# Linear attention's weights by pairs of heads, and sample attention's steps by twos, in a hybrid decoder layer on one core

## The chip, the core and the metric

One NeuronCore of a Trainium2 chip runs the whole layer as one program. Its engines run side by side: TensorE (PE; PEld is its weight load), VectorE (DVE), ScalarE (ACT), GpSimd (POOL) and SyncE (SP), which here issues most DMAs. The metric is the device time of one execution in microseconds (us), lower is better.

## What is computed

One layer serves 1024 prompt tokens and 8 sequences of 8 sample tokens (64 sample tokens, 1088 in all), model width 1024:

```python
h = macaron_half(x, ...)                 # SwiGLU feed-forward 1, half weight
fq, fk, fv, logf, gq, gk, gv, gg, log_a = project(rmsnorm(h), w_in, ...)
fo = fox_prompt(fq, fk, fv, logf)        # 8 heads x 64, softmax with forget bias
     # the sample tokens instead attend to 16 cached pages of 128 keys and values each
go = gla_prompt(gq, gk, gv, log_a)       # 4 heads, key 64, value 128, linear attention
h = h + rmsnorm(merge(fo, go, gg, ...))  # go is normed, times silu(gg); then w_out
y = macaron_half(h, ...)                 # feed-forward 2
```

In the linear attention the weight of key position s for query position t is the sum over the 64 key channels of `q[t] * k[s] * exp(b[t] - b[s])` for s <= t, with `b` the running sum of the log decay.

## The kernel before

**Projections by three products.** Activations and weights are split in a high and a low part (type fp32r), and every product is three matmuls a 128-row block of the inner dimension: `gemm` (line 210) for w_in, w_out and the gate and up halves of the feed-forwards, `down` (line 440) for the down half. One `gemm` over 512 tokens is 8 inner blocks of 3 matmuls. Weights come as blocks of 512 KB through `Feed`: two raw tiles, then three split ones (`wh`, `wl`), in the order of use.

**Background work in pieces.** Attention is a Python generator that the projections advance while they are written out. After each inner block, `tick` adds a planned time, 0.42e-3 us per matmul column, and for `rate` times that time it calls `piece`, which advances the generator to its next `yield`. A block over 512 tokens counts 3 x 512 x 0.42e-3 = 0.645 planned us. A planner then fixes each engine's order by priority (order of writing) and by when it believes operands to be there. What of the generator is left at a fixed place is written out at once by `finish_bg`.

**Stages.** (1) feed-forward 1; (2) w_in for the first 512 tokens; (3) `start3`: the rest of w_in, with prompt attention for tokens 0 to 511 beside it (`fox` over 16 pairs of a 256-query chunk and a head; `gla` over four tiles of 128 tokens, held back until `hook3`), rate RATE0 = 1.1, finished at `mid3`; (4) w_out for those tokens; (5) `start4`: feed-forward 2 for the first 512 tokens. Its groups G0 (two blocks of 128 hidden columns) and G1 to G4 (four blocks each) take gate and up first, then down. Beside them runs `second`: first `sample` at rate RATES = 1.1, then at RATE1 = 2.6 `fox` and `gla` for tokens 512 to 1023 and the sample tokens (`gla` tiles 4, 5, 8, 6, 7; 8 is the sample tile), taking turns by `together`, which yields after every step of either. At its end `second` loads the mixed heads back from DRAM (`mixd` to `p4.y`, line 1388) and splits them into `ub` in eight pieces. `mid4` calls `finish_bg` after G4's down, and (6) w_out for the last 576 columns starts there, which reads `ub`; (7) feed-forward 2 ends.

**Linear attention of one tile.** `gla_prep` makes for each of seven levels (64, 32, ... 1; three for the sample tile) the decays E, their exponential on ACT, and multiplies k into one half of each level's columns and q into the other (line 1166). `gla_mid` has for two levels at a time, and for each half e of the 128 partitions (two heads stand in a tile's two halves), the matmuls `pa` (line 1209) of 64 rows: stationary E's 128 columns, moving its 64 query columns. A masked copy puts them into `at` (line 1212). Then it yields. The operands are plain fp32, and the trace has two passes of each such matmul. `gla_post` multiplies with the values and the state, norms, and multiplies with `gg` (line 1280), which it loads at its start.

**Sample attention.** `sample` handles four pairs of sequences. `LEAD` pieces pass first; then come the steps, one to a piece: 16 key steps (K) and 16 value steps (V) a pair, each on 512 KB of cached pages (lines 837 and 875: four matmuls with 32 stationary columns, two passes each), five `turn` steps of transposes, and `scored`, `out`. K steps of the next pair alternate with V steps. Pages are fetched six steps ahead.

Of the kernel before, what the change touches and what calls it, by code (L numbers as in the profile page):

```python
# [8 lines left out]
F32 = mybir.dt.float32  # L9
# [4 lines left out]
ALU = mybir.AluOpType  # L14
# [4 lines left out]
P = 128  # L19
# [527 lines left out]
LEAD = 10  # L547
# [6 lines left out]
class StepA(Step):  # L554
    def setup_a(self):
        cp, nc = self.const, self.nc
        dr = self.dram
        self.qs = dr.tile([2, 4, P, T], F32, name="qs")
        self.ks = dr.tile([2, 4, P, T], F32, name="ks")
        self.vs = dr.tile([4, P, 2, KB, P], F32, name="vs")  # L560
        self.vss = dr.tile([4, 2, TS, P], F32, name="vss")
        self.augs = dr.tile([8, 2, TP], F32, name="augs")
        self.cns = dr.tile([2, 8, TS], F32, name="cns")
        self.afs = dr.tile([NB, 2, 8, NPG, P], F32, name="afs")
        self.gqs = dr.tile([2, P, T], F32, name="gqs")
# [6 lines left out]
        self.mixs = cp.tile([P, 4, TS], F32, name="mixs")  # L572
        self.gS = cp.tile([P, 2, P], F32, name="gS")
        self.cend = cp.tile([8, 4], F32, name="cend")

    def load_a(self):
        cp, nc, A = self.const, self.nc, self.A
        for nm, shape in (("wa2", [16, 256]), ("ba", [P, 2]), ("rst", [P, HALF + TS]), ("later", [P, P])):
            t = cp.tile(shape, F32, name=nm)
            nc.sync.dma_start(t, A[nm])  # L580
            setattr(self, nm, t)
        self.bf = cp.tile([40, 1], F32, name="bf")
        nc.sync.dma_start(self.bf[32:40, :], A["bf"])
# [67 lines left out]
    def gates(self, c0, n, pt):  # L651
# [5 lines left out]
        rs = self.rst[:, HALF:]  # L657
# [7 lines left out]
        for i in range(2):  # L665
            if i:
                yield 6.0
            z = aux("z2")
            nc.tensor.matmul(z[:, :n], self.wa2[:, i * P:(i + 1) * P], gz[:16, :n], start=True, stop=True)
            e, m = st(), st()  # L670
            nc.scalar.activation(out=e[:, :n], in_=z[:, :n], func=AF.Abs, bias=self.ba[:, i:i + 1])
            nc.scalar.activation(out=e[:, :n], in_=e[:, :n], func=AF.Exp, scale=-1.0)
            nc.scalar.activation(out=e[:, :n], in_=e[:, :n], func=AF.Ln, bias=1.0)
            nc.vector.tensor_scalar(m[:, :n], z[:, :n], self.ba[:, i:i + 1], 0.0, op0=ALU.add, op1=ALU.min)
            nc.vector.tensor_tensor(out=m[:, :n], in0=m[:, :n], in1=e[:, :n], op=ALU.subtract)
            b = e
            nc.vector.tensor_tensor_scan(out=b[:, :npr], data0=self.rst[:, :npr], data1=m[:, :npr], initial=0.0, op0=ALU.mult, op1=ALU.add)
            if npr < n:
                nc.vector.tensor_tensor_scan(out=b[:, npr:n], data0=rs, data1=m[:, npr:n], initial=0.0, op0=ALU.mult, op1=ALU.add)
            nc.sync.dma_start(self.gbs[i][:, c0:c0 + n], b[:, :n])  # L680
# [43 lines left out]
    def past_bias(self, pool):  # L724
# [4 lines left out]
        nc.sync.dma_start(idx, A["pt_col"])  # L729
        lg, inc = [big(pool.tile([P, T], F32, name=self.uid("pb"), tag="sg", bufs=2)) for _ in range(2)]  # L730
# [9 lines left out]
        nc.tensor.matmul(of[:, :8], self.later, tot, start=True, stop=True)  # L740
# [17 lines left out]
    def sample(self, X, ps):  # L758
# [5 lines left out]
        tmp = lambda nm, shape, dt: X.tile(shape, dt, name=nm, tag="ob", bufs=2)  # L764
        self.pgt = cst("pgt", [1, P], I32)
# [131 lines left out]
        def paged(kind, p, t):  # L897
            n = len(pages)
            pages.append((kind, p, t))
            steps.append(lambda: (key_step if kind == "K" else value_step)(n, p, t))  # L900

        def scored(p):
            steps.append(lambda: new_keys(p))
            steps.append(lambda: (soft(p), queries(p + 1) if p + 1 < NP else None))

        for t in range(16):
            paged("K", 0, t)
        scored(0)
        for p in range(NP):
            ks = list(range(16)) if p + 1 < NP else []  # L910
            if p == 0:
                for t in ks[:2]:
                    paged("K", 1, t)
                ks = ks[2:]
            for j in range(5):
                steps.append(lambda p=p, j=j: turn(p, j))
# [49 lines left out]
RATES = 1.1  # L966
# [18 lines left out]
class StepB(StepA):  # L985
    def setup_b(self, B):
# [18 lines left out]
        nc.gpsimd.memset(self.qe, 0.0)  # L1005
        self.qb = []
# [117 lines left out]
    def gla_prep(self, ti, B):  # L1124
# [46 lines left out]
    def gla_mid(self, ti, B):  # L1171
# [29 lines left out]
        for l0 in range(0, L, 2):  # L1201
            ls = list(range(l0, min(l0 + 2, L)))
            for e in range(2):
                pa = self.aux("pa", P, 2, 2, 64)
                vw = lambda x, l: x.rearrange("p a (k m) -> p a k m", m=2 * lev[l])[:, :, :, lev[l]:]
                for l in ls:
                    x = E[64 * e:64 * e + 64, l, :, :n]
                    for a in range(2):
                        nc.tensor.matmul(pa[:n, l - l0, a, :n // 2], x[:, a], vw(x, l)[:, a], start=True, stop=True)  # L1209
                for l in ls:  # L1210
                    mk = vw(self.lmask[:n, l + 7 - L:l + 8 - L, :n], l)[:, 0].unsqueeze(1).to_broadcast([n, 2, n // (2 * lev[l]), lev[l]])
                    nc.vector.copy_predicated(vw(at_[:, 2 * e:2 * e + 2, :], l), mk, pa[:n, l - l0, :, :n // 2].rearrange("p a (k m) -> p a k m", m=lev[l]))
                yield
        self.tile_in[ti] = (v, at, kn, el)

    def gla_post(self, ti, put, B):
# [8 lines left out]
        gg = self._gl(B, "gg", self.ggs, 4, ti * P, n)  # L1225
# [53 lines left out]
        nc.vector.scalar_tensor_tensor(out=o[:, :, :n], in0=o[:, :, :n], scalar=self.gnorm[:, :1], in1=rb[:, :, :n], op0=ALU.mult, op1=ALU.mult)  # L1279
        nc.gpsimd.tensor_tensor(out=o[:, :, :n], in0=o[:, :, :n], in1=gg, op=ALU.mult)  # L1280
# [116 lines left out]
    def whole(self):  # L1397
# [10 lines left out]
        UB, close_ub = self.pool("UB", side="right")  # L1408
        self.ub = [UB.tile([P, KB, H1N], F32R, name=f"ub{i}") for i in range(2)]
# [165 lines left out]
def consts():  # L1575
# [5 lines left out]
    r=np.ones((128,512+64),np.float32); r[:,0:512:128]=0; r[:,512::8]=0; c['rst']=r  # L1581
# [62 lines left out]
```

## Time and profile before

| | before |
|---|---|
| median of 3 runs | 2444.93 us (2437.53 to 2446.8) |
| profiled execution, its own time | 2454.03 us |
| its span, first to last instruction | 2452.3 us |
| mean granted TensorE clock | 0.983 |
| busy, share of the span | PE 98%, PEld 86%, DVE 48%, ACT 35%, POOL 15% |

Busy time is the time in which at least one instruction of an engine is open; matmuls overlap one another, so what a matmul costs is read from the distance of two starts and not from its own duration.

### The profile page before, as it was taken

The page shows a single profiled execution, that of the slowest core. Times are in us where ns is not written, and L with a number is a line of the kernel's source. Part 1 is how long each engine was busy: PE and PEld are TensorE (multiplying, and loading weights), DVE is VectorE, ACT ScalarE, POOL GpSimd, SP SyncE. Part 2 cuts the span into 40 slices and gives each one's busy share as a digit, 9 for nine tenths or more (in the row PEclk, how much of TensorE's full clock was granted, in tenths as well). Part 3 has the DMA queues.
Part 4 walks back from the last instruction along what each step waited for, and adds up shares of the span by engine and source line. Part 5 has one row for each costly group of instructions (what it writes and reads, how often), then busy time and mean ns, then how long its engine had stood idle before and what let it go on. Part 6 is the DMA issues. An engine that isn't in the chain of part 4 may idle for free.

```text
span 2452.3 us, 39759 instructions
## 1 busy us (share of the span) xinstructions
PE 2392.2 (98%) x15688; PEld 2105.6 (86%) x15688; DVE 1170.8 (48%) x2300; ACT 863.0 (35%) x1582; POOL 359.2 (15%) x418
## 2 busy tenths in 40 slices
PE   7999999999999999999999999999999999999997
PEld 7799999999999879899997555578888999999997
DVE  7223232232347765555565232357776674333345
ACT  5311211111134545555354222245454543222222
POOL 3000000000003220000124354710000321000001
PEclk9999999999999999799999999999999999999999
DMA  3111111111134576464256899856544534222222
GB/s 123 65 48 44 44 43 44 47 49 44 50 97 147 178 239 204 139 187 146 80 177 217 305 334 324 276 164 173 169 126 161 178 115 159 87 83 82 87 71 89
DMA packets 177083, 330.71 MB, mean 135 GB/s; under 512 B 25153, under 2 KB 100610, under 8 KB 176898
## 3 DMA queue, kind: packets, MB, share of 16 engines
q1 hardware_dynamic: 165234, 289.90, 36.9%
q0 software_dynamic: 11664, 38.28, 4.5%
q8 instruction: 124, 2.03, 0.3%
q14 instruction: 61, 0.50, 0.1%
HBM read 284.42 MB, written 43.69 MB: 134 GB/s over the span
## 4 chain that ended last, share of the span: by engine, by line
PE 38%; issue 4%; DVE 3%; DMA 2%; POOL 2%; ACT 1%; SPq 0%; POOLq 0%; ACTq 0%; DVEq 0%
PE mm L210 20%; PE mm L440 10%; PE sp L837 1%; PE po L875 1%; DMA wr<-in_wout 1%; PE pa L1209 1%; PE tp L1065 1%; PE po L1080 1%; DVE wl L146 1%; POOL pr L798 1%; ACT wh L145 1%; POOL y L328 0%; PE s L1047 0%; DMA pr<-in_cv,rows 0%; PE s L1048 0%
## 5 line engine op out<-in xcount | busy, mean ns | idle before, releaser
L210 PE MATMUL mm<-ub,wh 128*128 128x320 f32 (+2 forms) x3776 | 774.6, 300 | 0.1
L210 PE MATMUL mm<-ua,wh 128*128 128x512 f32 (+2 forms) x2288 | 641.8, 366 | 5.4 <-ACT wh L145 2.7
L210 PEld LDWEIGHTS mm<-ub,wh 128*128 128x128 f32 (+1 forms) x3776 | 610.5, 190 | 10.7 <-issue 3.7
L146 DVE TENSOR_TENSOR wl<-wr,wh 128x1024 fp32r<-128x1024 f32 (+1 forms) x294 | 357.8, 1217 | 449.0 <-ACT wh L145 442.2
L145 ACT CAST wh<-wr 128x1024 fp32r<-128x1024 f32 (+1 forms) x294 | 301.2, 1025 | 723.6 <-PE mm L210 309.3
L210 PE MATMUL mm<-ub,wl 128*128 128x320 f32 (+1 forms) x1872 | 554.8, 297 | 0.5 <-DVE wl L146 0.5
L210 PEld LDWEIGHTS mm<-ua,wh 128*128 128x128 f32 (+1 forms) x2288 | 400.4, 192 | 82.7 <-issue 23.3
L210 PE MATMUL mm<-ua,wl 128*128 128x512 f32 (+1 forms) x1136 | 408.8, 361 | 1.2 <-DVE wl L146 1.2
L210 PEld LDWEIGHTS mm<-ub,wl 128*128 128x128 f32 x1872 | 356.0, 190 | 0.7 <-DVE wl L146 0.7
L440 PE MATMUL mm<-hl,wh 128*128 128x256 f32 (+4 forms) x1088 | 354.3, 326 | 0.0
L440 PE MATMUL mm<-hh,wh 128*128 128x256 f32 (+2 forms) x1040 | 340.0, 328 | 1.0 <-DVE y L450 1.0
L440 PE MATMUL mm<-hh,wl 128*128 128x256 f32 (+2 forms) x1040 | 332.8, 321 | 0.0
L210 PEld LDWEIGHTS mm<-ua,wl 128*128 128x128 f32 x1136 | 217.4, 192 | 35.5 <-issue 2.7
L450 DVE TENSOR_TENSOR y<-y,mm 128x256 f32<-128x256 f32 (+2 forms) x272 | 130.0, 503 | 215.5 <-PE mm L440 215.0
L440 PEld LDWEIGHTS mm<-hl,wh 128*128 128x128 f32 (+1 forms) x1088 | 206.0, 189 | 22.1 <-issue 11.4
L440 PEld LDWEIGHTS mm<-hh,wh 128*128 128x128 f32 x1040 | 196.5, 189 | 23.2 <-issue 11.1
L224 POOL TENSOR_TENSOR ss<-ss,sq 128x256 f32<-128x256 f32 (+1 forms) x46 | 44.0, 959 | 1149.8 <-ACT sq L220 1149.2
L440 PEld LDWEIGHTS mm<-hh,wl 128*128 128x128 f32 x1040 | 196.6, 189 | 14.8 <-issue 3.7
L379 DVE TENSOR_TENSOR sg<-mm,sg 128x256 f32<-128x256 f32 (+4 forms) x112 | 55.7, 498 | 185.8 <-PE mm L210 184.3
L798 POOL DMA_INDIRECT pr<-in_cv,rows x128 | 128.3, 1003 | 98.1 <-PE po L875 41.2
L145 ACT CAST hh<-sg 128x320 fp32r<-128x320 f32 (+2 forms) x128 | 62.6, 489 | 213.1 <-DVE sg L379 170.0
L373 ACT ACTIVATE sg<-mm 128x256 f32<-128x256 f32 (+4 forms) x112 | 49.1, 439 | 143.8 <-PE mm L210 143.6
(243 smaller groups left out, 2309.5 us busy)
## 6 DMA issues: line engine op xcount, KB each, us to landing
wr<-in_wgu SPq DMA_DIRECT2D x137, 512.0 KB
wr<-in_wd SPq DMA_DIRECT2D x60, 512.0 KB
pr<-in_ck SPq DMA_DIRECT2D x112, 256.0 KB
wr<-in_win SPq DMA_DIRECT2D x50, 512.0 KB
wr<-in_wout SPq DMA_DIRECT2D x32, 512.0 KB
h<-y SPq DMA_DIRECT2D x12, 512.0 KB
x<-h SPq DMA_DIRECT2D x24, 256.0 KB
wr<-in_wd SPq DMA_DIRECT2D x20, 256.0 KB
```

What stands on the lines that cost most here:

```text
L145: self.nc.scalar.copy(hi, src)
L146: self.nc.vector.tensor_tensor(out=lo, in0=src, in1=hi.bitcast(F32), op=ALU.subtract)
L210: nc.tensor.matmul(out, a, x[:, k, o:o + n], start=(k == 0 and j == 0), stop=(k == KB - 1 and j == len(ops) - 1))
L224: (nc.gpsimd if odd else nc.vector).tensor_tensor(out=s, in0=s, in1=sq[:, :n], op=ALU.add)
L373: nc.scalar.activation(out=t, in_=src, func=AF.Silu)
L379: nc.vector.tensor_tensor(out=out, in0=u, in1=t, op=ALU.mult)
L440: nc.tensor.matmul(pds[e], a, b, start=(i == 0 and j == 0), stop=(i == len(g) - 1 and j == len(ops) - 1))
L450: nc.vector.tensor_tensor(out=yk, in0=yk, in1=pds[e], op=ALU.add)
L798: nc.gpsimd.indirect_dma_start(out=raw[:, i], out_offset=None, in_=A["ck" if kind == "K" else "cv"].rearrange("g p n -> (g p) n"), in_offs ...
L837: nc.tensor.matmul(sp[32 * a:32 * a + 32, 256 * hf:256 * hf + 256], qz[p % 2][:, a, s, :], raw[:, :, a * P:(a + 1) * P], start=False, stop ...
L875: nc.tensor.matmul(po[r], pT[:, t, r], raw[:, :, a * P:(a + 1) * P], start=(t == 0), stop=False)
L1065: nc.tensor.transpose(tp[:, k * P:(k + 1) * P], p[:, (k0 + k) * P:(k0 + k + 1) * P], self.ident)
```

## The change

- **Linear attention.** A new tile `qd` (128 x 7 x 2 x 2 x 64, zeroed once on POOL) takes q times decay, each half of the partitions in columns of its own, zero elsewhere. `pa` then takes both heads of a tile in one matmul of 128 rows and 128 moving columns. The loop over e, its copies and its yield go: half as many matmuls, masked copies and yields. The multiplication with q is two instructions a level instead of one.
- **gg** is loaded just ahead of its use, into the buffer that the norm used before it; one more yield stands between.
- **Sample.** K and V steps go out two to a piece where they alternate, the first pair's K steps two by two, and K steps beside a `turn` in its piece. LEAD 10 becomes 6, RATES 1.1 becomes 0.6.
- **Memory.** Small constants move to other pools; `rst` shrinks, so that the gate scan over 512 columns is made in two halves.

```diff
-LEAD = 10
+LEAD = 6
...
-            nc.vector.tensor_tensor_scan(out=b[:, :npr], data0=self.rst[:, :npr], data1=m[:, :npr], initial=0.0, op0=ALU.mult, op1=ALU.add)
+            for o in range(0, npr, 256):
+                nc.vector.tensor_tensor_scan(out=b[:, o:o + 256], data0=self.rst[:, :256], data1=m[:, o:o + 256], initial=0.0, op0=ALU.mult, op1=ALU.add)
...
-            steps.append(lambda: (key_step if kind == "K" else value_step)(n, p, t))
+            return lambda: (key_step if kind == "K" else value_step)(n, p, t)
+
+        def piece(*fns):
+            steps.append(lambda: [f() for f in fns])
...
-        for t in range(16):
-            paged("K", 0, t)
+        for t in range(0, 16, 2):
+            piece(paged("K", 0, t), paged("K", 0, t + 1))
         scored(0)
         for p in range(NP):
             ks = list(range(16)) if p + 1 < NP else []
             if p == 0:
-                for t in ks[:2]:
-                    paged("K", 1, t)
-                ks = ks[2:]
+                piece(*[paged("K", 1, ks.pop(0)) for _ in range(2)])
             for j in range(5):
-                steps.append(lambda p=p, j=j: turn(p, j))
-                if ks and j % 2 == 0:
-                    paged("K", p + 1, ks.pop(0))
+                tn = lambda p=p, j=j: turn(p, j)
+                piece(*([paged("K", p + 1, ks.pop(0))] if ks and j % 2 == 0 else []), tn)
             for t in range(NPG):
-                paged("V", p, t)
+                fs = [paged("V", p, t)]
                 if ks:
-                    paged("K", p + 1, ks.pop(0))
+                    fs.append(paged("K", p + 1, ks.pop(0)))
+                    piece(*fs)
                     if not ks:
                         scored(p + 1)
-            steps.append(lambda: None)
-            steps.append(lambda p=p: out(p))
+                else:
+                    piece(*fs)
+            piece()
+            piece(lambda p=p: out(p))
...
-RATES = 1.1
+RATES = 0.6
...
+        self.qd = cst("qd", [P, 7, 2, 2, 64])
+        nc.gpsimd.memset(self.qd, 0.0)
...
-            for src, s in ((k, slice(0, m)), (q, slice(m, 2 * m))):
-                ev = vw(E[:, l, :, :n])[:, :, :, s]
-                nc.vector.tensor_tensor(out=ev, in0=ev, in1=vw(src)[:, :, :, s], op=ALU.mult)
+            el, kv, qv = vw(E[:, l, :, :n]), vw(k), vw(q)
+            nc.vector.tensor_tensor(out=el[:, :, :, :m], in0=el[:, :, :, :m], in1=kv[:, :, :, :m], op=ALU.mult)
+            for e in range(2):
+                r = slice(64 * e, 64 * e + 64)
+                o = self.qd[r, l, :, e, :n // 2].rearrange("p a (k m) -> p a k m", m=m)
+                nc.vector.tensor_tensor(out=o, in0=el[r, :, :, m:], in1=qv[r, :, :, m:], op=ALU.mult)
...
-            for e in range(2):
-                pa = self.aux("pa", P, 2, 2, 64)
...
+            pa = self.aux("pa", P, 2, 2, 2, 64)
...
+            for l in ls:
+                for a in range(2):
+                    nc.tensor.matmul(pa[:n, l - l0, :, a, :n // 2], E[:, l, a, :n], self.qd[:, l, a, :, :n // 2], start=True, stop=True)
...
-        gg = self._gl(B, "gg", self.ggs, 4, ti * P, n)
...
+        gg = self._gl(B, "gsq", self.ggs, 4, ti * P, n)
+        yield
         nc.gpsimd.tensor_tensor(out=o[:, :, :n], in0=o[:, :, :n], in1=gg, op=ALU.mult)
```

## Rows read from the trace of the kernel before

**Rows 1.** The page, parts 1 and 2: busy time; the span in 40 slices.

```profile
PE 2392.2 (98%) x15688; PEld 2105.6 (86%) x15688; DVE 1170.8 (48%) x2300; ACT 863.0 (35%) x1582; POOL 359.2 (15%) x418
...
PE   7999999999999999999999999999999999999997
```

**Rows 2.** Timeline of PE (start, duration, instructions merged): bursts of `pa` between projections.

```profile
1202.92 0.40 PE L210 MATMUL mm<-ua,wh 128*128 128x256 f32 x2
1203.16 0.28 PE L210 MATMUL mm<-ua,wl 128*128 128x256 f32 x1
1203.37 1.10 PE L1209 MATMUL pa<-E 64*128 64x64 f32 x8
1204.40 0.38 PE L210 MATMUL mm<-ua,wh 128*128 128x256 f32 x1
```

**Rows 3.** Line 1209's own view: passes, durations min/median/max, first and last start.

```profile
L1209 PE MATMUL pa<-E x472: 219/272/473, 1000.6 to 1831.3; 64*128 64x64 f32 x150, 64*64 64x32 f32 x8
```

**Rows 4.** Timeline of PE: eight fp32 passes with 128 rows and 128 moving columns.

```profile
1832.75 1.06 PE L1229 MATMUL go<-at,gv 128*128 128x128 f32 x8
1833.64 1.03 PE L1237 MATMUL go<-qe,gS 128*128 128x256 f32 x4
```

**Rows 5.** Timeline of PE in sample attention: a pair, then a single step.

```profile
1394.76 0.39 PE L210 MATMUL mm<-ua,wl 128*128 128x512 f32 x1
...
1396.09 0.74 PE L210 MATMUL mm<-ua,wh 128*128 128x512 f32 x2
...
1396.90 0.63 PE L210 MATMUL mm<-ua,wh 128*128 128x512 f32 x2
1397.37 0.39 PE L210 MATMUL mm<-ua,wl 128*128 128x512 f32 x1
1397.69 0.64 PE L875 MATMUL po<-pr,pT 128*32 128x256 f32 x8
1398.26 0.73 PE L210 MATMUL mm<-ua,wh 128*128 128x512 f32 x2
```

**Rows 6.** Busy time by stretch: length, busy (instructions) by engine, clock, DMA share, GB/s.

```profile
1460.00:1480.00 20.00, 20.00 (x146) 12.43 (x139) 7.13 (x11) 3.74 (x4) 10.94 (x12) 1.00 0.98 350
1480.00:1500.00 20.00, 20.00 (x162) 11.87 (x161) 6.05 (x13) 5.38 (x8) 9.71 (x10) 1.00 0.96 350
```

**Rows 7.** Groups of instructions, DVE and POOL: count, busy us, mean ns, idle before.

```profile
L1212 DVE COPY_PREDICATED at<-lmask,pa 128x128 f32<-128x128 uint8 x112 | 36.7, 337 | 44.9 <-PE pa L1209 44.0
...
L1166 DVE TENSOR_TENSOR E<-E,gq 128x128 f32<-128x128 f32 x56 | 15.8, 282 | 0.1
...
L1187 DVE TENSOR_TENSOR at<-pd,ident 128x256 f32<-128x256 f32 x16 | 6.4, 416 | 5.6 <-PE pd L1186 5.4
...
L1280 POOL TENSOR_TENSOR o<-o,gg 128x512 f32<-128x512 f32 (+1 forms) x9 | 11.0, 1228 | 59.4 <-issue 26.7 <-DVE o L1279 25.7 <-DMA v<-vs 7.0
```

**Rows 8.** Timeline of all engines: the end of `second`, its DMAs, the first splits.

```profile
1862.05 0.93 PE L1080 MATMUL po<-pT,v 128*128 128x256 f32 x7
...
1863.02 0.36 ACT L1082 COPY pl<-po 64x256 f32<-64x256 f32 x1 [1.93 <-PE po L1080]
...
1863.87 0.33 SPq L1370 DMA_DIRECT2D mixd<-mo  x1
...
1870.62 2.18 ACT L145 CAST ub<-y 128x512 fp32r<-128x512 f32 x4 [2.11 <-DMA y<-mixd]
...
1871.27 1.89 DVE L146 TENSOR_TENSOR ub<-y,ub 128x512 fp32r<-128x512 f32 x3 [1.42 <-ACT ub L145]
```

**Rows 9.** Groups of PE, 1862.8 to 1866.9: G4's gate and up matmuls behind the last `po`.

```profile
L210 PE MATMUL mm<-ua,wh 128*128 128x512 f32 x12 | 3.8, 394 | 0.0
L210 PE MATMUL mm<-ua,wl 128*128 128x512 f32 x6 | 2.3, 390 | 0.0
```

**Rows 10.** Busy time by stretch, as rows 6: G4's down; two slow stretches.

```profile
1867.00:1888.70 21.70, 21.70 (x97) 17.98 (x96) 15.66 (x21) 9.37 (x14) 0.00 (x0) 1.00 0.70 245
...
999.70:1027.00 27.30, 26.93 (x100) 23.07 (x100) 10.46 (x27) 14.45 (x26) 0.13 (x1) 0.50 0.32 100
1027.00:1054.00 27.00, 27.00 (x197) 25.49 (x197) 21.86 (x80) 15.98 (x36) 2.81 (x6) 1.00 0.56 174
1207.90:1218.00 10.10, 10.10 (x38) 8.76 (x38) 2.88 (x6) 2.32 (x5) 0.00 (x0) 0.50 0.08 26
```

**Rows 11.** Timeline of PE: an idle stretch of PE, and matmuls behind it.

```profile
1270.56 0.46 PE L210 MATMUL mm<-ub,wh 128*128 128x320 f32 x2
1270.85 0.31 PE L210 MATMUL mm<-ub,wl 128*128 128x320 f32 x1
1275.35 0.61 PE L239 MATMUL ncol<-ones,ss 128*128 128x2 f32 x4 [4.19 <-DVE ss L224]
1275.82 0.61 PE L210 MATMUL mm<-ub,wh 128*128 128x320 f32 x2
1276.22 0.47 PE L210 MATMUL mm<-ub,wl 128*128 128x320 f32 x1
```

More of the change, by code (lines that the diff above doesn't have):

```diff
@@ L571, in setup_a @@
         nc.vector.memset(self.zero, 0.0)
-        self.mixs = cp.tile([P, 4, TS], F32, name="mixs")
         self.gS = cp.tile([P, 2, P], F32, name="gS")
@@ L576, in load_a @@
     def load_a(self):
-        cp, nc, A = self.const, self.nc, self.A
-        for nm, shape in (("wa2", [16, 256]), ("ba", [P, 2]), ("rst", [P, HALF + TS]), ("later", [P, P])):
-            t = cp.tile(shape, F32, name=nm)
+        nc, A = self.nc, self.A
+        for nm, shape in (("wa2", [16, 256]), ("ba", [P, 2]), ("rst", [P, 256 + TS])):
+            t = self.UB.tile(shape, F32, name=nm)
             nc.sync.dma_start(t, A[nm])
             setattr(self, nm, t)
-        self.bf = cp.tile([40, 1], F32, name="bf")
+        self.bf = self.UB.tile([40, 1], F32, name="bf")
         nc.sync.dma_start(self.bf[32:40, :], A["bf"])
@@ L656, in gates @@
         aux = lambda nm: self.ps.tile([P, 512], F32, name=self.uid(nm), tag="aux", bufs=self.naux)
-        rs = self.rst[:, HALF:]
+        rs = self.rst[:, 256:]
         gz = st()
@@ L729, in past_bias @@
         nc.sync.dma_start(idx, A["pt_col"])
+        later = pool.tile([P, P], F32, name="later", bufs=1)
+        nc.sync.dma_start(later, A["later"])
         lg, inc = [big(pool.tile([P, T], F32, name=self.uid("pb"), tag="sg", bufs=2)) for _ in range(2)]
@@ L739, in past_bias @@
         of = self.mm(512)
-        nc.tensor.matmul(of[:, :8], self.later, tot, start=True, stop=True)
+        nc.tensor.matmul(of[:, :8], later, tot, start=True, stop=True)
         nc.vector.tensor_tensor(out=inc, in0=inc, in1=of[:, :8].unsqueeze(2).to_broadcast([P, 8, P]), op=ALU.add)
@@ L764, in sample @@
         tmp = lambda nm, shape, dt: X.tile(shape, dt, name=nm, tag="ob", bufs=2)
+        self.mixs = cst("mixs", [P, 4, TS])
         self.pgt = cst("pgt", [1, P], I32)
@@ L899, in paged @@
             pages.append((kind, p, t))
-            steps.append(lambda: (key_step if kind == "K" else value_step)(n, p, t))
+            return lambda: (key_step if kind == "K" else value_step)(n, p, t)
+        def piece(*fns):
+            steps.append(lambda: [f() for f in fns])
         def scored(p):
-            steps.append(lambda: new_keys(p))
-            steps.append(lambda: (soft(p), queries(p + 1) if p + 1 < NP else None))
-        for t in range(16):
-            paged("K", 0, t)
+            piece(lambda: new_keys(p))
+            piece(lambda: soft(p), *([lambda: queries(p + 1)] if p + 1 < NP else []))
+        for t in range(0, 16, 2):
+            piece(paged("K", 0, t), paged("K", 0, t + 1))
         scored(0)
@@ L1202, in gla_mid @@
             ls = list(range(l0, min(l0 + 2, L)))
-            for e in range(2):
-                pa = self.aux("pa", P, 2, 2, 64)
[L1205 to L1213, printed above, removed]
+            pa = self.aux("pa", P, 2, 2, 2, 64)
+            vw = lambda x, l: x.rearrange("p a (k m) -> p a k m", m=2 * lev[l])[:, :, :, lev[l]:]
+            for l in ls:
+                for a in range(2):
+                    nc.tensor.matmul(pa[:n, l - l0, :, a, :n // 2], E[:, l, a, :n], self.qd[:, l, a, :, :n // 2], start=True, stop=True)
+            for l in ls:
+                mk = vw(self.lmask[:n, l + 7 - L:l + 8 - L, :n], l)[:, 0].unsqueeze(1).to_broadcast([n, 4, n // (2 * lev[l]), lev[l]])
+                nc.vector.copy_predicated(vw(at_, l), mk, pa[:n, l - l0, :, :, :n // 2].rearrange("p e a (k m) -> p (e a) k m", m=lev[l]))
+            yield
         self.tile_in[ti] = (v, at, kn, el)
@@ L1279, in gla_post @@
         nc.vector.scalar_tensor_tensor(out=o[:, :, :n], in0=o[:, :, :n], scalar=self.gnorm[:, :1], in1=rb[:, :, :n], op0=ALU.mult, op1=ALU.mult)
+        gg = self._gl(B, "gsq", self.ggs, 4, ti * P, n)
+        yield
         nc.gpsimd.tensor_tensor(out=o[:, :, :n], in0=o[:, :, :n], in1=gg, op=ALU.mult)
@@ L1408, in whole @@
         UB, close_ub = self.pool("UB", side="right")
+        self.UB = UB
         self.ub = [UB.tile([P, KB, H1N], F32R, name=f"ub{i}") for i in range(2)]
@@ L1580, in consts @@
     c['smask']=np.where((t//8==2*p_+s_)&(t%8<=q_),0,-1e30).astype(np.float32)
-    r=np.ones((128,512+64),np.float32); r[:,0:512:128]=0; r[:,512::8]=0; c['rst']=r
+    r=np.ones((128,256+64),np.float32); r[:,0:256:128]=0; r[:,256::8]=0; c['rst']=r
     s=np.zeros((128,128),np.float32)
```

## The prediction

> **What bounds the kernel.** I read the page first. PE is busy for 98% of the span and for nine tenths or more in all but the outermost slices [rows 1]; no other engine passes 48%. PE's program is one long line of projections with attention set between them, so the time is the sum of start-to-start distances on PE plus the few places where it waits. A change counts by the PE passes it removes, by the switches between projections and background bursts, and by waits it makes or hides. So the second view is PE's timeline inside the bursts that the change touches, and the third is the place where background work must be finished before projections may go on: the end of `second`.
>
> **The `pa` matmuls.** Eight passes of `pa` stand between projections. From the last matmul ahead to the first behind it is 1204.40 - 1203.16 = 1.24 us; the distance of two such projection matmuls is 0.12 (two in 1202.92 to 1203.16), so the burst costs 1.12 us [rows 2]. The code has 28 such matmuls for each of eight tiles and 12 for the sample tile, 236, and the trace has 472 passes [rows 3]: two each. What does a pass of 128 rows and 128 moving columns cost? `go` at line 1229 has that shape in the same type: eight take 1833.64 - 1832.75 = 0.89 us to the next start, 0.111 each [rows 4]. The eight of `pa` are open for 1.10 us against 1.06 for those of `go`, so the 64-row passes are no cheaper: per pass 0.11 too, and 1.12 - 8 x 0.111 = 0.23 for going in and out. The change makes 236 passes of 472 and 34 bursts of 68 (eight to four a tile, four to two for the sample tile).
> Sum: 236 x 0.111 = 26.2 us, plus 34 x 0.23 = 7.8 if each lost burst stood alone. Beside other attention work the switch stays, since the other work makes it. Bounds 26 and 34 us; I take 32, nearer the upper end, because the bursts of rows 2 stand alone.
>
> The Trainium skill ("TensorE: Matmul & The Clock Gate", Part 3, on packing small matmuls) says that matmuls on different row strips of the array run side by side, so two 64-row halves would already cost what one 128-row matmul costs, and merging them would give no more than the switches. The trace speaks against it here: all eight passes of a burst use the same half, since a yield stands between the two values of e, and they come 0.11 us apart [rows 2]. By the rule the sum below would end near 2449 us.
>
> **Work around `pa`.** On DVE the q products become two a level: 7 more a tile at 0.282 us, +2.0 us. The masked copies go from 14 at 0.337 us (4.7 us) to 7 of twice the width; the nearest row of that size out of PSUM takes 0.416 us, twice the small one would be 0.674, so 7 cost 2.9 to 4.7 us [rows 7]. Net 0.2 to 2.0 us more a tile, 2 to 16 us over eight on an engine that idles half the time [rows 1]. PE hides it: nothing, and 2 us a tile if `pa` waited. Zeroing `qd`, the moved constants and the scan in two halves are a few instructions of about a microsecond ahead of stages in which PE has projections: nothing.
> The load of gg is now issued when PE has done the norm's product. On SP the weight loads behind it wait as long; three split blocks stand ahead, and a block lasts 24 projection matmuls (2.9 us at 0.12), so that is covered. On POOL the product at line 1280 waits for the landing, with the next tile's E and kd steps behind it; POOL is busy 15% [rows 1] and idled 59 us ahead of these nine products already [rows 7]. Nothing; if the cover failed, a few us a tile.
>
> **Sample steps by twos.** A V step alone costs 1398.26 - 1397.37 = 0.89 us less one projection distance of 0.23 (two in 1396.90 to 1397.37), 0.66. A V and a K together, which the planner has already put side by side there, cost 1396.09 - 1394.76 = 1.33 less 0.23 = 1.10 [rows 5]. So a merge saves 0.22 us. Before, 24 bursts hold such a pair (rows 5 show one); after, the code makes 37, and nine K steps join a `turn`: about 24 merges more with the switches at the turns, 5 us.
> But pairs ask for pages faster. At 0.6 a planned us a pair comes every 1.67 planned us. G4's down has 21.7/97 = 0.224 us a matmul [rows 10] where the plan has 0.215, so that is 1.74 us of projections plus 1.10: 2.84 us for two steps, 1.05 MB, 370 GB/s; with one weight block (24 matmuls and three pairs, 8.7 us) 430 GB/s. The trace has 350 GB/s at a DMA share of 0.96 to 0.98 [rows 6]. Thirteen pairs in a row last 37 us and fall 3.0 MB short; six steps fetched ahead are 3.1 MB. It just covers. So I take -5 us; bounds -10 (no page is waited for, the slower second half also frees DMA) and +27 (the stock isn't there: 8 us in each of three runs of pairs, and the clock).
>
> **The end of `second`.** I count pieces. Sample: before 10 + 164, after 6 + 109. At their rates B1, the stage behind it, is set up at planned 159.6 us and now at 193.1, of the 271.8 that G0 to G4 have. Then `together` has 114 steps of `fox` and 104 of `gla` (9 + 6 + 6 a tile, 20 the sample tile), now 114 + 91, and 12 pieces load and split `ub`. Before: 159.6 + 218/2.6 = 243.4, and all done at 247.9, just ahead of G4's down at 251.2. The trace agrees: G4's down is 97 matmuls in 21.7 us with none of the background work between [rows 10], and it hides everything behind the last `po`. After: 78.7 x 2.6 = 204 pieces are handed out, `together` alone needs 205. So the last `fox` step and all 12 pieces fall to `finish_bg`, and w_out has nothing to hide them.
> Price: `po` ends at 1862.98; `mixd` is written at 1863.87, `ub` is cast from 1870.62, and its first low part is done at 1871.27 + 0.68 = 1871.95 [rows 8]: 9.0 us. Before that, `fox` lags behind the order of writing: its last step was written after block 52 of 64 of G4's gate and up, with 36 matmuls to go, and at its end 18 were left [rows 9]: 18 x 0.224 = 4 us. With 23 steps of `fox` alone at the end in place of 10 the lag can only grow; I take 7. Then the clock: after an idle stretch of 4.2 us two matmuls took 0.40 us (1275.82 to 1276.22) against 0.29 ahead of it [rows 11]; at worst as in the long slow stretch, 100 matmuls where the next as long had 197 at full clock [rows 10], 13 us. I take 3. Together +19 us, bounds 0 (the planner finds other work) and 29.
>
> **Slow clock.** Two long stretches at a granted 0.50 (1.2 GHz) lie where linear attention works: 27.3 us from 999.7, 10.1 from 1207.9 [rows 10]. The second holds the last tile's `pa`, which `mid3` pushed out among w_out; with 12 pieces less in that stage it moves ahead of `mid3`. The first loses 13 us by the count of matmuls above, so the second some 13 x 10.1/27.3 = 5; I take half of it, -2, since `pa` still runs somewhere, and let the first stay. Bounds -18 and 0.
>
> **Sum.** -32 - 5 + 19 - 2 = -20 us. The profiled execution has 2454.03 us, so 2434 in a profile; it stands 9 us above the median of the runs, 2444.93, so **2425 us** there.
>
> **Rivals.**
> (a) The end of `second` is hidden after all, because the planner finds other projections for that place or `fox` keeps up: 2425 - 19 = 2406. For it: the planner does reorder, as the pair in rows 5 shows. Against: the next weights stand behind w_out's in the order of use. Chance 0.20.
> (b) Pages run dry in the three runs of pairs. Price +32 against the -5, from the point at which a pair per 2.84 us uses more than 350 GB/s plus what was fetched ahead: 2425 + 32 = 2457, slower. For it: rows 6. Against: no wait for pages stands in that stretch before. Chance 0.14.
> (c) The long slow stretch near 1000 us goes too, since fewer, fuller passes stand in it: -13, 2412. Chance 0.08.
> (d) The change doesn't do what it says, 128 rows cost as two halves: -32 becomes -8, 2449. The skill's rule, which would end there too, stands above. Chance 0.06.
> (e) My own: 0.52.
>
> **Numbers.** A difference under about 0.5% (12 us) can't be told from none here. Faster by more: below 2432.7. My own case with its spread of some 9 us lies there four times in five: 0.52 x 0.8 = 0.42, with (a) and (c) 0.70, less some for mixtures of (b) with the others: 0.66. Slower by more, above 2457.2: half of (b) and its mixtures, 0.10. Same: 0.24. The range reaches from below (a) to just short of (b): 2400 to 2450.
>
> **What the new profile would show.** Line 1209 with 236 passes of 128 rows, eight still some 1.1 us: right; 2 us: (d). Busy time of PE in stage (3) down by half of 1209's. An idle stretch of PE of 15 us or more ahead of the first w_out matmul on `ub`, the last `po` just ahead of it: right; none: (a). PE waiting on `pr` among the pairs: (b). If neither the idle stretch nor 236 passes show, my count of pieces or of passes is wrong.

## The result

The changed kernel takes **2426.76 us** (median of 7 runs, 2413.35 to 2429.78); the kernel before, run beside it, 2440.35 (7 runs, 2436.63 to 2448.72). That is 13.6 us faster in the medians. The ratio that is estimated from all of these runs is 0.9926, with a 95% interval of 0.9898 to 0.9953, which would be 18 us, between 11 and 25; so the size of the gain is known no better than that. The profiled execution of the changed kernel took 2429.76 us with a span of 2428.0, 24.3 us less than that of before, which lay high among its runs. Runs of one kernel differ by their granted clock: the profiled run of after had 0.984, its fastest run (2413.35) 0.989.

Page of after, parts 1 and 2, answering [rows 1]: busy time, and the 40 slices of PE and its clock.

```profile
PE 2346.4 (97%) x15452; PEld 2074.3 (85%) x15452; DVE 1174.9 (48%) x2302; ACT 862.7 (36%) x1582; POOL 361.2 (15%) x420
...
PE   7999999999999999999998999999997999999997
...
PEclk9999999999999999999998999999998999999998
```

PE has 236 instructions less, just the `pa` passes, and two slices between the outermost where it isn't full: the 22nd, at eight tenths, and the 31st, 1821 to 1882 us, at seven. The new line of `pa`, answering [rows 3], is all 236 passes with 128 rows (64 columns in the sample tile):

```profile
L1218 PE MATMUL pa<-qd,E x236: 222/275/377, 1000.9 to 1797.1; 128*128 128x128 f32 x112, 128*64 128x64 f32 x6
```

A burst of it between projections, PE's timeline as in [rows 2]:

```profile
1009.13 0.40 PE L210 MATMUL mm<-ub,wh 128*128 128x256 f32 x2
1009.36 0.28 PE L210 MATMUL mm<-ub,wl 128*128 128x256 f32 x1
1009.48 1.05 PE L1218 MATMUL pa<-qd,E 128*128 128x128 f32 x8
1010.29 0.48 PE L210 MATMUL mm<-ub,wh 128*128 128x256 f32 x2
```

From the last projection matmul ahead to the first behind it: 1010.29 - 1009.36 = 0.93 us, less one distance of 0.12 makes 0.81. The 64-row burst cost 1.12 [rows 2], for half of the same work. A pass comes 0.111 us behind the one before in both; going in and out differs. From the start of the last pass to the next projection matmul it is 0.03 us here, where the 64-row passes had 0.20 (in 26 of 28 such bursts of before at full clock, and in all 11 of after). Going in, the last projection matmul ahead and the first pass of a 64-row burst took 0.14 us more together.

The end of `second`, all engines, answering [rows 8] and the first of [rows 10] (start, duration, in brackets the idle time ahead and what ended it):

```profile
1839.01 0.40 PE L440 MATMUL mm<-hh,wl 128*128 128x512 f32 x1
...
1843.37 0.55 PE L1073 MATMUL tp<-ident,p 128*128 128x128 f32 x3 [2.61 <-DVE pT L146]
...
1848.28 3.50 PE L1088 MATMUL po<-pT,v 128*128 128x256 f32 x15
...
1852.67 0.32 SPq L1380 DMA_DIRECT2D mixd<-mo  x1
1853.09 1.86 SPq L1398 DMA_DIRECT2D y<-mixd  x2
...
1859.30 2.18 ACT L145 CAST ub<-y 128x512 fp32r<-128x512 f32 x4 [7.12 <-DMA y<-mixd]
...
1859.97 1.31 PE L210 MATMUL mm<-ub,wh 128*128 128x256 f32 x4 [8.19 <-ACT ub L145]
```

G4's down ends at 1839 and w_out begins at 1859.97, **21 us** later, where before there were 0.2. But PE isn't idle for all of it: 8.4 us are attention's own last passes, which PE would have to run elsewhere too, and 12.6 are idle.

Where the time went, in start-to-start distances on PE with idle time apart. The stretch is the last 1152 projection matmuls ahead of w_out (feed-forward 2 from its first 512-wide block on, with the later part of `sample` and all of the second attention).

| us | before | after |
|---|---|---|
| start of the stretch | 1360.4 | 1330.6 |
| `pa` in it | 30.4 | 13.4 |
| projections in it | 301.2 | 296.2 |
| idle PE in it | 5.5 | 22.5 |
| slow clock in it (length) | 10.2 | 21.6 |
| length | 528.3 | 529.4 |
| start of w_out | 1888.7 | 1860.0 |
| w_out to the end | 563.5 | 568.0 |

So 29.8 us are won ahead of the stretch; 61.5 us there were at a granted 0.50 in before, and 37.5 in after. Inside it, the 17.0 us that `pa` gives are eaten by 17.0 us more of idle PE.

### The profile page after: what moved, and what is told of

It reads as the page before. It is cut to its first block, busy times and chain, and to the rows that moved or that the text cites. A ratio compares the mean times of both kernels' runs of the same rounds, so it can differ in the third digit from the quotient of the medians.

```text
span 2428.0 us, 39284 instructions
## 1 busy us (share of the span) xinstructions
PE 2346.4 (97%) x15452; PEld 2074.3 (85%) x15452; DVE 1174.9 (48%) x2302; ACT 862.7 (36%) x1582; POOL 361.2 (15%) x420
## 4 chain that ended last, share of the span: by engine, by line
PE 76%; DVE 9%; DMA 4%; ACT 4%; issue 4%; POOL 2%; SPq 1%; POOLq 0%; DVEq 0%; ACTq 0%
PE mm L210 46%; PE mm L440 21%; PE po L878 2%; DVE wl L146 1%; PE sp L840 1%; DMA wr<-in_wout 1%; ACT wh L145 1%; PE tp L1073 1%; PE po L1088 1%; DVE qd L1177 1%; DVE fm L1060 1%; DVE pT L146 1%; PE pa L1218 1%; POOL y L328 1%; POOL ss L224 0%
## 5 line engine op out<-in xcount | busy, mean ns | idle before, releaser
L145 ACT CAST wh<-wr 128x1024 fp32r<-128x1024 f32 (+1 forms) x294 | 301.2, 1025 | 743.1 <-PE mm L210 314.7
L210 PEld LDWEIGHTS mm<-ua,wh 128*128 128x128 f32 (+1 forms) x2288 | 401.2, 192 | 79.5 <-issue 23.9
```

Of the source, the lines that this page charges most:

```text
L145: self.nc.scalar.copy(hi, src)
L210: nc.tensor.matmul(out, a, x[:, k, o:o + n], start=(k == 0 and j == 0), stop=(k == KB - 1 and j == len(ops) - 1))
```

## Experiments

The times of one batch are compared by the kernel before that ran beside it, whose median was 2442.0 in the first batch (e), 2461.6 in the second (f) and 2468.5 in the third (g). The changed kernel ran again in the third batch only. In the first two, a distance from it is taken over batches, and is rough: by medians or by the two ratios to before it comes out 3 to 6 us apart in the first, and some 20 in the second, where before itself stood 20 us higher.

**One half of the change at a time.** The first kernel has the new linear attention and the sample attention of before:

```diff
-LEAD = 6
+LEAD = 10
...
-            piece(paged("K", 0, t), paged("K", 0, t + 1))
...
+            paged("K", 0, t)
...
-RATES = 0.6
+RATES = 1.1
```

> The new linear attention (pairs of heads, gg loaded late, new pools) with the old sample attention: LEAD 10, RATES 1.1, one step to a piece. By the count of pieces the second background stage is set up at planned 159.6 us as before, needs 205 + 13 pieces, and is done near 243, ahead of G4's down, which hides the way of its result through DRAM. Theory A (pa gives 32 to 38 us, and some 19 us of that are lost again at the end of the background work): 2440 - 36 = 2404 us, no idle stretch of PE over 3 us ahead of the second w_out. Theory B (pa itself gives no more than the 14 us by which the whole change is faster): 2427 us.

Measured: 2417.67 us, ratio 0.9902 (0.9875 to 0.993), 9 us below the changed kernel by medians and 6 by the ratios, whose intervals overlap; between the two theories. No gap: w_out begins 0.2 us after G4's down. In the stretch of the table idle PE is 12.7 us, all of it in attention itself.

The second has the new sample attention alone:

```diff
...
-            pa = self.aux("pa", P, 2, 2, 2, 64)
...
+            for e in range(2):
+                pa = self.aux("pa", P, 2, 2, 64)
...
+                yield
```

> The old linear attention with the new sample attention (LEAD 6, RATES 0.6, steps by twos). The second stage is set up at planned 193.1 us, 204 pieces are handed out, together needs 218: 14 steps of prompt attention, two heads, and the 12 pieces behind them stand after the last projection. Theory A: the pairs give 5 us, the exposed end costs 20 us as in the changed kernel and two heads without projections beside them some 15 more: 2440 - 5 + 35 = 2470 us, slower than before. Theory B (the end costs little, the sample part is worth what is left): 2435 us.

Measured: 2459.64 us, ratio 1.0074 (1.0044 to 1.0104): slower. With 218 steps in `together` and 204 pieces handed out, the gap is 30.5 us, 16.0 of it idle. The half of the change that was to save 5 us on PE costs some 18 on balance, and only the other half, with fewer pieces, makes the whole faster.

**The gap by dose.** Attention's rate in the second stage raised, and nothing else:

```diff
-RATE1 = 2.6
+RATE1 = 3.6
```

> The changed kernel with RATE1 = 3.6 in place of 2.6, nothing else: pieces of the second stage are handed out faster, so that all 218 are out at planned 193.1 + 218/3.6 = 253.7 us, with 18 planned us of G4's down behind them. Theory A (the idle stretch of about 20 us ahead of w_out comes from too few pieces and goes when they are handed out in time): 2427 - 20 = 2407 us and no idle stretch over 3 us there. Rival C (prompt attention's own chain of score, softmax, transpose and split can't go faster; PE waits for it inside the stage in place of at its end): 2420 to 2427 us, with waits of transposes and products spread over the stage.

Measured: 2414.05 us, ratio 0.9896 (0.9868 to 0.9924), 12.7 us below the changed kernel by medians, 7 by the ratios, whose intervals overlap. The gap is 0.2 us, but idle PE inside the second attention rose from 9.6 to 12.3, so that in the whole stretch of the table it fell by 10.0 (22.5 to 12.5). At 3.0 in place of 3.6:

> The changed kernel with RATE1 = 3.0 in place of 2.6: between the changed kernel and the run at 3.6. All 218 pieces are out at planned 193.1 + 218/3.0 = 265.8 us, 6 planned us ahead of w_out. Theory A (the idle stretch is the lag of prompt attention plus 9 us of DRAM and splitting, less the projections left behind the last piece): about 21 - 6 = 15 us between the last matmul of G4's down and w_out's first in place of 21, less if the lag shrinks; time 2420 us. Rival (the stretch has a fixed cause that 3.6 merely avoided by another order): 21 us still, 2427 us.

Measured: 2427.76 us, ratio 0.985 (0.979 to 0.9909), gap 12.9 us. So 2.6, 3.0 and 3.6 give 21, 12.9 and 0.2 us: the gap is what is left over when the pieces run short, as counted. Its price is another matter. The time at 3.0 can't be set against 2.6 over batches, but idle PE in the stretch is still 22.1 us there: 9.4 of the gap's 12.9 us are idle, and what else was won came back as waits ahead of it. The same rate 3.6 beside the changed kernel, on another chip:

> The changed kernel with attention's rate in the second stage 3.6 in place of 2.6 and nothing else, on the chip of this batch: 0.9896 of the kernel before as first measured (0.987 to 0.992), no gap ahead of w_out, and about 12 us of idle PE inside the second-stage attention. It stands here to be set against the same rate with the q products on GpSimd.

Measured: 2425.32 us, against 2433.71 for the changed kernel beside it: 8.4 us, and here the runs don't overlap (2421.79 to 2428.4 against 2430.01 to 2436.55). Idle PE in the stretch fell by 9.6 us (24.3 to 14.7). So hiding the gap gave 7 to 13 us: about what idle PE fell by, and not the gap's length.

**The rate of the sample steps.**

```diff
-RATES = 0.6
+RATES = 0.7
```

> The changed kernel with RATES = 0.7 in place of 0.6, nothing else. Sample attention's pieces end earlier, the second stage is set up near planned 164 us and is done near 248, ahead of G4's down, so that its end is hidden; a pair of page steps is asked for every 1.43 planned us in place of 1.67. Theory A (the end costs about 20 us, of which the two runs without it gave 9 and 13 in the medians): 2414 us, no idle stretch ahead of w_out. Rival (b) (pages run dry in the runs of pairs: some 460 GB/s asked for, 350 seen): the gain is eaten by waits of PE for pages, 2427 us or more, with more idle time of PE put down to the page DMAs than the changed kernel has.

Measured: 2431.48 us, ratio 0.9853 (0.9805 to 0.9901), 4 us above the kernel at RATE1 3.0 beside it, with runs that overlap (2423.91 to 2439.06 against 2426.75 to 2433.86). The forecast 2414 did not come. The end is hidden (0.2 us), and what it gave comes back as waits: idle PE from the start of feed-forward 2 to attention 17.2 us against 9.7, inside the second attention 14.3 against 8.6. PE's waits in the first of these stretches; pages are the row of `pr`, and the kernel at RATES 0.6 and RATE1 3.0 had 1.0 us there:

```profile
PE sp L840 <- DMA pr<-in_ck: 3.0, 4, 1.5
PE tp L865 <- DVE mixs L895: 2.5, 1, 2.5
PE mm L440 <- ACT y L448: 2.3, 1, 2.3
```

**Single steps in place of pairs**, all else as changed, at RATES 0.9, so that sample attention lasts about as long:

```diff
-LEAD = 6
+LEAD = 10
...
-                    fs.append(paged("K", p + 1, ks.pop(0)))
-                    piece(*fs)
+                    paged("K", p + 1, ks.pop(0))
...
-RATES = 0.6
+RATES = 0.9
```

> The changed kernel with sample steps one to a piece (LEAD 10) at RATES = 0.9, so that the second stage is set up at planned 193 us as in the changed kernel: what the steps by twos are worth by themselves. Theory A (a merged pair saves 0.22 us, some 24 merges): 2427 + 5 = 2432 us. Rival D (pairs ask for pages too fast and lose in waits what they save in switches): 2427 us or less.

Measured: 2431.03 us, ratio 0.9953 (0.9934 to 0.9971): 4.3 us above the changed kernel. The two intervals overlap at 0.9934 to 0.9953, so the size is rough. On PE's timeline this kernel has 9 bursts that hold a V and a K step, the changed one 26; its sample bursts cost 2.8 us more, and its gap ahead of w_out has 14.5 us of idle PE in place of 12.6.

**The price of a pass.** Every `pa` matmul issued twice, into the same place:

```diff
-                    nc.tensor.matmul(pa[:n, l - l0, :, a, :n // 2], E[:, l, a, :n], self.qd[:, l, a, :, :n // 2], start=True, stop=True)
+                    for _ in range(2):
+                        nc.tensor.matmul(pa[:n, l - l0, :, a, :n // 2], E[:, l, a, :n], self.qd[:, l, a, :, :n // 2], start=True, stop=True)
```

> The changed kernel with each pa matmul issued twice (the second writes the same values again): 236 passes of 128 rows more, no other switch. Theory A (a pass of 128 rows and 128 columns costs 0.111 us on a PE that bounds the kernel): 2427 + 26 = 2453 us. Rival (PE waits at those places for the vector engine anyway, so that passes are free there): 2427 to 2435 us.

Measured: 2455.25 us, ratio 0.9961 (0.9933 to 0.9989), 27.5 us above the kernel at RATE1 3.0 beside it and a span 27.0 above that of the changed kernel. The line of `pa` took 25.8 us more on PE (50.6 against 24.8 without idle time). 236 passes more, 26 to 27 us: 0.11 a pass, all of it on the path.

**64-row passes of both halves as neighbours.** The kernel before, with the two halves' matmuls alternating and a PSUM tile for each:

```diff
+            pas = [self.aux("pa", P, 2, 2, 64) for _ in range(2)]
...
+            for l in ls:
+                for a in range(2):
+                    for e in range(2):
+                        x = E[64 * e:64 * e + 64, l, :, :n]
+                        nc.tensor.matmul(pas[e][:n, l - l0, a, :n // 2], x[:, a], vw(x, l)[:, a], start=True, stop=True)
...
-                yield
...
+            yield
```

> The kernel before with the matmuls of the two partition halves one behind the other in one burst: for each level and head pair first rows 0 to 63, then rows 64 to 127, into two PSUM tiles; one yield for both halves as in the change, sample attention as before, the copies not merged. It has the 472 passes of 64 rows of the kernel before. Theory A (passes cost 0.11 us each whatever their rows): 26 us of the change's gain don't come, only the switches fall away: 2442 - 7 = 2435 us, 16 passes open for 2.0 us. Rival (the Trainium skill, TensorE: Matmul & The Clock Gate, Part 3: matmuls on different row strips run side by side): 16 passes take little more than 1 us and the time is that of the run with the new linear attention alone, 2418 us.

Measured: 2458.88 us, ratio 0.9973 (0.9944 to 1.0001): neither forecast time. The planner moved more than half of the passes apart again, into bursts of eight or four of one half; of the 12 bursts of sixteen that are left, nine alternate throughout. The line of `pa` on PE fell to 53.7 us from 64.4, but the profile has 110 us at a granted 0.5 where before has 86, and its runs had a granted clock of 0.977 to 0.983 against 0.976 to 0.989. So the time can't decide between the two theories; the bursts have to. PE's timeline shows both kinds:

```profile
1001.68 1.10 PE L1209 MATMUL pa<-E 64*128 64x64 f32 x8 [0.58 <-ACT kn L1192]
...
1184.85 0.28 PE L210 MATMUL mm<-ub,wl 128*128 128x256 f32 x1
1185.06 1.11 PE L1209 MATMUL pa<-E 64*128 64x64 f32 x16
1186.10 0.50 PE L210 MATMUL mm<-ub,wh 128*128 128x256 f32 x2
```

Where sixteen alternate they are open for 1.11 us, no longer than eight of one half, and the burst costs 1186.10 - 1184.85 - 0.12 = 1.13 us against 1.12 for eight in [rows 2]. In the nine bursts two passes of opposite halves start 6 to 14 ns apart, mostly 7, and the next two 0.11 us behind them.

**Who holds up attention.** The changed kernel once more, then with its q products on GpSimd, then that with rate 3.6.

> The changed kernel once more, on the chip of this batch, so that the next three kernels can be set against it. Expected ratio to the kernel before 0.993 (0.990 to 0.995 as measured first), PE idle inside the second-stage attention near 10 us, and about 21 us between the last matmul of feed-forward 2's last down group and the first of w_out.

```diff
-                nc.vector.tensor_tensor(out=o, in0=el[r, :, :, m:], in1=qv[r, :, :, m:], op=ALU.mult)
+                nc.gpsimd.tensor_tensor(out=o, in0=el[r, :, :, m:], in1=qv[r, :, :, m:], op=ALU.mult)
```

> The changed kernel with the two q products a level on GpSimd instead of VectorE (118 instructions of 282 ns leave VectorE). Theory: in the second stage PE waits for the transposed weights of prompt attention because their splits stand behind these products on VectorE; without them PE's idle time inside that attention falls from 9.6 us towards the 3.5 us of the kernel before, and the time by about 6 us against the changed kernel on the same chip (ratio to before 0.990 against 0.993). Rival: GpSimd is slower at each product, the pa matmuls wait for the products instead, and the time stays or grows by 5 us or more. The gap ahead of w_out should stay near 21 us under both.

> As the kernel with the q products on GpSimd, and attention's rate in the second stage 3.6 in place of 2.6, so that all of it is handed out before w_out. Theory: the gap ahead of w_out goes (21 us to 0.2), and with VectorE relieved less of it comes back as waits for the transposed weights: 5 us less than the changed kernel at rate 3.6 alone, some 18 us less than the changed kernel, ratio to before 0.986. Rival: what comes back at the higher rate is not VectorE's queue, but the chain through ScalarE's exponentials; then it ends level with rate 3.6 alone, 0.9896.

Measured: 2433.71 us (ratio 0.9877, 0.9807 to 0.9947), 2431.61 (0.9866, 0.9797 to 0.9936) and 2418.77 (0.982, 0.9749 to 0.9891). The intervals are wide because before itself ran from 2450 to 2481 us on that chip. Moving the products alone makes no difference that can be told. Idle PE inside the second attention was 8.3 us in the changed kernel repeated and 9.5 with the products on GpSimd. PE's waits inside the second attention, first the changed kernel repeated, then with the products on GpSimd (total us, times, longest):

```profile
PE tp L1073 <- DVE pT L146: 4.6, 8, 1.2
```

```profile
PE rb L1286 <- DVE gsq L1283: 4.2, 1, 4.2
PE tp L1073 <- DVE pT L146: 3.6, 7, 0.9
```

One us of the wait that I blamed on them goes, and a new one of 4.2 comes. GpSimd's timeline at that place, in the same kernel:

```profile
1650.25 5.22 POOL L1177 TENSOR_TENSOR qd<-E,gq 64x128 f32<-64x128 f32 x10 [3.38 <-ACT E L1167]
1655.55 1.05 POOL L1280 TENSOR_TENSOR rv<-rv,mhalf 128x4 f32<-128x4 f32 x1
```

Ten products take 5.22 us there, 0.52 each where VectorE took 0.28, and the norm's `rv` stands behind them: the rival's mechanism, for one tile. At rate 3.6 the kernel with the products on GpSimd was 6.6 us below the one without, but the runs overlap (2416.64 to 2425.46 against 2421.79 to 2428.4), and not where I expected it: idle PE in the stretch of the table is 14.9 us in one and 14.7 in the other, and the 9.1 us by which w_out starts earlier are there already at the start of the stretch. What gave them isn't settled. The three kernels without a gap that stood furthest below the changed one (this one by 14.9 us beside it; over batches, rate 3.6 alone by 12.7 and new linear attention alone by 9.1) can't be ranked among each other.

## Why the prediction was right, and where its steps failed

I had forecast 2425 us, -20 from the median shown; 2426.76 came, -13.6 against the median of the runs beside it and -18 by the ratio. The direction and the two large terms, `pa` and the end of `second`, rest on the right mechanisms. That the time came within 2 us is luck: before's median was 4.6 us lower beside it, runs of after spread over 16 us, and the parts didn't all come as sized.

**`pa`: right, too small.** I took -32, bounds 26 and 34. All of the line on PE fell from 64.4 to 26.1 us (1.3 of it idle), -38.3, above the upper bound. Two corrections to that are of like size. 46 of the 472 passes of before lie in slow stretches and take 11.1 us, where as many others take 5.8; none of after does. And what going in costs stands on the projection matmul ahead and not in this line: 0.1 us at each of 52 bursts of before, 0.03 at 25 of after, 4.5 us. The 26.2 for the passes hold (doubling them cost 26 to 27). The term that failed is going in and out: I let the remaining 34 bursts keep their 0.23 us, but a 128-row burst costs 0.81 us, eight passes less 0.08, so these win as well.

**Row halves: the trace's reading held, and so does the rule where it applies.** [rows 2] had eight passes of one half, and there merging halves the number of full-price passes, as forecast. Where both halves alternate, sixteen passes cost as much as eight. By the rule of the Trainium skill ("TensorE: Matmul & The Clock Gate", Part 3) that matmuls on different row strips run side by side, the alternating bursts agree (1.13 us for sixteen) and the bursts of the kernel before don't call on it. Rival (d) is out: 0.81 us, not two.

**Work around `pa`: wrong.** I put it at nothing, because VectorE "idles half the time" [rows 1]. VectorE's sum was right: 1170.8 us became 1174.9 over the whole span. What failed is that PE hides it. The half is the mean over 2452 us; in the stretch where the second attention runs VectorE is busier. Busy time of PE, PEld, DVE, ACT and POOL there, in before, then after, then new sample alone, then products on GpSimd:

```profile
1617.00:1888.50 271.50, 268.02 (x1547) 219.63 (x1546) 199.48 (x468) 145.12 (x246) 24.30 (x39) 0.99 0.55 160
```

```profile
1619.00:1839.00 220.00, 209.85 (x1219) 171.99 (x1218) 177.54 (x434) 127.54 (x219) 23.13 (x39) 0.98 0.56 162
```

```profile
1640.00:1865.00 225.00, 223.05 (x1314) 181.76 (x1313) 167.66 (x427) 121.94 (x210) 21.80 (x38) 0.98 0.57 157
```

```profile
1620.00:1840.00 220.00, 210.02 (x1218) 170.55 (x1216) 166.35 (x372) 127.10 (x219) 58.54 (x101) 0.98 0.57 162
```

In the same order, VectorE is busy for 73% (199.48 / 271.50), 81%, 75% and 76% of it, and idle PE is 3.5, 9.6, 1.4 and 9.5 us. The share isn't the whole cause, since the last of these has before's share and after's idle time; the waits say more. The wait that grew, in before and in after:

```profile
PE tp L1065 <- DVE pT L146: 1.8, 4, 0.7
```

```profile
PE tp L1073 <- DVE pT L146: 4.8, 9, 1.1
```

`tp`, the transposes' PSUM tile, has one buffer, so PE's next transpose waits until the split has read it. The split comes late because VectorE is at something else. One such place in after:

```profile
1655.37 0.28 DVE L1177 TENSOR_TENSOR qd<-E,gq 64x128 f32<-64x128 f32 x1
1655.68 0.43 DVE L1091 TENSOR_TENSOR mo<-po,pl 64x256 f32<-64x256 f32 x1
1656.03 0.28 DVE L1177 TENSOR_TENSOR qd<-E,gq 64x128 f32<-64x128 f32 x1
1656.34 0.69 DVE L146 TENSOR_TENSOR pT<-tp,pT 128x512 fp32r<-128x512 f32 x1
...
1657.09 0.33 PE L1073 MATMUL tp<-ident,p 128*128 128x128 f32 x1 [1.15 <-DVE pT L146]
```

It is something in the new linear attention that does it: all kernels with it have 3.6 us or more of this wait there, the two others with the old one have 0.8 (row halves) and none (new sample alone). It isn't the lost cover of PE, since doubling `pa` on PE left it at 5.9 us. The q products are a part, 1 to 2 us (4.6 to 3.6, and 7.4 to 5.5 at rate 3.6). The yield that went isn't it by itself: the kernel with row halves has one yield for both halves too, and 0.8 us of this wait. Of the rest, the masked copies (0.517 us each in place of 0.337) and the late load of gg weren't tried apart: that stays open. The price is 5 to 6 us (9.6, and 8.3 when repeated, less 3.5).

**Sample steps: the size came, the merges didn't.** -5 forecast; the bursts net of one projection distance each fell from 104.2 us in 118 to 98.6 in 106, -5.6. But I had that from some 24 merges more on PE, and PE's timeline has 25 bursts with a V and a K step in before and 26 in after, though the code makes 37 pairs: the planner fixes the order on PE, not the piece. Only about 2 us of the 5.6 are passes and switches (96.4 to 94.4); the rest is idle PE inside these bursts (8.1 to 4.4 us). That the sum fits is luck. The kernel with single steps, 4.3 us slower, shows what 17 such bursts fewer cost together with a longer gap, and not a gain over before. A pair, V and K passes interleaved by the planner as in [rows 5], costs 1356.78 - 1355.44 - 0.23 = 1.11 us, where I had 1.10:

```profile
1355.44 0.40 PE L210 MATMUL mm<-ua,wh 128*128 128x512 f32 x1
1355.77 0.40 PE L878 MATMUL po<-pr,pT 128*32 128x256 f32 x1
1355.78 0.42 PE L840 MATMUL sp<-pr,qz 128*32 128x256 f32 x3
...
1356.78 0.50 PE L210 MATMUL mm<-ua,wh 128*128 128x512 f32 x1
```

Rival (b) didn't come: PE waited 3.2 us for pages in all, in before 4.0. At RATES 0.7 it was 3.0 in the stretch, a tenth of the price I had given it.

**The end of `second`: the mechanism right, the price too high.** The count of pieces held, and the gap of 21 us is close to 9 + 7 + 3. But in the 7 of lag I priced PE passes that are only moved. What it costs is the idle part, 12.6 us, and the times of the runs that hide it say 7 to 13, with the slower clock behind it (10.2 us at 0.5 from 1855.5) inside and what came back as waits taken off. Rival (a) needed another rate.

**Slow clock: one of two as forecast.** The stretch near 1208 went as I had it: in after the last tile's `pa` ends near 1177, ahead of w_out at 1189, and no slow stretch is there. In the kernel with the old linear attention and the new sample steps `pa` still stands behind w_out's start, and 10.3 us at 0.5 begin at 1200.5. The long one near 1000, which I let stay, is gone in after, 3.4 us at 1016 in place of 27.3, as in rival (c), worth 13 us there. But that isn't a gain of the new passes as such: the same kernel with the old linear attention hasn't it either, and that with row halves has 30.7 us of it. And other stretches came in: over the whole span 85.9 us were at 0.5 in before and 79.5 in after. PE worked 70.2 and 57.8 us of these, which at half the speed is some 6 us, an estimate. What decides on these stretches stays open.

**The sum again**, from the whole record of PE in the two profiles, start to start with idle time apart: `pa` -39.5 (64.4 to 24.8), projections -11.0, other attention +4.9, idle PE +21.4 (43.8 to 65.2). That is -24.2, the difference of the profiles. Other attention stands for all that is neither `pa` nor projection, and the slow clock is inside these terms. Of the idle time, 12.6 us are the gap and 6.1 waits inside the second attention. In the medians -13.6 is left: the profile of before lay 13.7 us above its median in the runs beside after, that of after 3.0 above its own. Against my sum, `pa` gave some 6 us more than I took and the end cost 6 less, both to the same side. Against them stand the waits on VectorE, which I had put at nothing, and 4.4 us more idle PE outside the stretch of the table, which stays unexplained. That the forecast came near is in part these errors making up for one another.

## What to carry to other kernels

Read the busy share of an engine in the stretch where the new work falls, not on the page: 48% was 73% there, and four fifths after the change. When a change thins out background work that a plan hands out by count, count the pieces against the places again and set the rate anew; here that was worth 7 to 13 us, about half of the change or more. Look also at what PE's timeline makes of the pieces: 37 pairs in the code were 26 on PE, where 25 stood before. And price a gap by its idle time, not by its length.

## What the chip showed that I had not expected

The first projection matmul behind a burst of `pa` starts 0.20 us after the start of the burst's last pass when that has 64 rows and 0.03 us when it has 128, and going in costs 0.14 us more for 64 rows. And two fp32 passes on opposite row halves, neighbours on PE and writing different PSUM tiles, start 6 to 14 ns apart, so that sixteen take 1.11 us, as long as eight of one half.
